# The last channel block of a depthwise convolution moved to diagonal matrices on TensorE, and LayerNorm operations pinned by block

## The chip, the cores and the metric

One NeuronCore of one Trainium2 chip. The metric is the device time of one execution in microseconds (us). Engines: TensorE (PE) multiplies matrices, VectorE (DVE) and ScalarE (ACT) work element by element, GpSimd (POOL) does small operations and issues some transfers, SyncE (SP) issues the other transfers.

## The reference

One layer of a decoder on 512 tokens and 16 learned meta tokens in front of them, 1024 channels, float32. A mixing sub-layer: RMSNorm; one input projection whose columns go to a Mamba-2 state-space group (SSD, 16 heads, chunks of 128) and to a Conformer convolution group; the outputs of both, 2048 channels, pass one output projection, and the result is added to the stream. A channel sub-layer: RMSNorm, then retrieval over 128 x 128 experts (PEER). A last RMSNorm; the meta tokens are dropped. The part that the change touches:

```python
def conformer_conv(u, conv_w, conv_b, ln_g, ln_b):
    a, g = jnp.split(u, 2, axis=-1)
    h = causal_depthwise_conv(a * jax.nn.sigmoid(g), conv_w, conv_b)   # width 31, 1024 channels
    hf = h.astype(jnp.float32)
    mu = jnp.mean(hf, axis=-1, keepdims=True)
    var = jnp.mean(jnp.square(hf - mu), axis=-1, keepdims=True)
    hn = (hf - mu) * lax.rsqrt(var + EPS) * ln_g.astype(jnp.float32) + ln_b.astype(jnp.float32)
    return jax.nn.silu(hn).astype(u.dtype)
```

## The kernel before, in words

The program is one straight line of instructions; each engine's order is fixed when the program is built, by a list scheduler that runs a simulated time line. `early(n)` raises the priority of what stands in it by n, `late(n)` lowers it. Every matrix product is done as three matmuls in float32r (`mm3`, lines 160 to 162): each factor is split into a high part and a low remainder, and high x high, high x low and low x high are summed in PSUM. Lines 160, 161 and 162 in the profile are therefore those of all products.

Weights: `wload` (line 167) loads a raw block of 1 MB through SP's queue into one of two places. `wsplit` (line 176) copies it on ACT as the high part (line 184), again with its sign turned (line 185), and adds the raw block to that copy by an accumulating transfer on POOL's queue (line 186): the low part. The split parts too have two places, used in turn; a place is free when PE has done the matmuls on the block that was in it.

Input projection (lines 588 to 597): blocks z, x and c run in the order of the list `ORDER`, whose last entries are c6 and c7. `x_block` feeds SSD; `ssd(g)`, four groups of five chunks, runs with priority 2000 on all engines. `c_block(k)` (line 406) is one block of 128 convolution channels with all 528 tokens: two projections, the gate (tanh form of the sigmoid), `gl` = 14 zeros and 528 gated values, then the convolution with lowered priority: one ACT scaling (line 420) and 30 taps on DVE (line 422), each adding a shifted `gl` times a column of weights to the block's 512 columns. Then the mean of block 0 (`crow`) is taken off, and the sums `sumd` and `sumq` over blocks are kept for LayerNorm (lines 424 to 441); block 7 enters the statistics on its own (`sq7`).

SSD's results of groups 0 to 2 go through memory (`yD`) and are transposed and split into the left factors of the output projection (`y_group`, `y_split`: line 620 on PE, 626 on ACT, 627 on DVE; priority 300). `out_part([0])` and `out_part([1])` project SSD's 1024 channels, each in two halves of 512 output columns and 96 matmuls; line 653 adds a finished half to the stream. Between them and `out_part([2, 3])`, which projects the convolution's 1024 channels, stands LayerNorm (lines 672 to 696, priority 500): sums over channels by matmuls with ones (line 676), a few small operations, two matmul broadcasts to rows (line 402), and for each block k two DVE operations (691, 692), the swish and the high copy on ACT (693, 695), and the low part on DVE (696). These parts are written to the places `hl(k)`, which the left factors of `out_part([0])` (k = 0 to 3) and `out_part([1])` (k = 4 to 7) held. Behind `out_part([2, 3])` come the second RMSNorm (lines 701 to 714), the PEER queries and scores, and two long loops over experts (`down`, `up_mm`), also products in three matmuls.

Of the kernel before, what the change touches and what calls it, by code (L numbers as in the profile page):

```python
# [9 lines left out]
F32 = mybir.dt.float32  # L10
# [5 lines left out]
AF = mybir.ActivationFunctionType  # L16
OP = mybir.AluOpType
# [25 lines left out]
TB = 8  # L43
ORDER = "z0 c0 x4 c1 x5 x6 c2 x7 x0 z1 x1 c3 c4 z2 x2 c5 z3 x3 c6 c7".split()
YP = 300
MO = (0, 1, -1, 2, 3)


# [2 lines left out]
S_CW, S_CB, S_LG, S_LB, S_SW, S_SB = 0, 248, 256, 264, 272, 336  # L51
# [4 lines left out]
def consts_array():  # L56
    c = np.zeros((128, C_N), np.float32)
    p = np.arange(128)
    c[:, C_ID:C_ID + 128] = np.eye(128)
    c[:, C_TRI:C_TRI + 128] = p[:, None] <= p[None, :]  # L60
    c[:, C_IOTA:C_IOTA + 128] = p[None, :]
    c[:, C_I50:C_I50 + 50] = np.arange(50)[None, :]
    return c


def pack(inputs):
    g = {k: np.asarray(v) for k, v in inputs.items()}
    ac = np.ascontiguousarray
    w_in = g["w_in"][0]
    zc, xbc, dtc, ca, cg = 0, 1024, 3072, 3088, 4112  # L70
    blocks = []
    for k in range(1, 4):
        blocks.append(w_in[:, zc + 256 * k:zc + 256 * k + 256])
    for k in range(8):
        blocks.append(w_in[:, xbc + 256 * k:xbc + 256 * k + 256])
    for k in range(8):
        blocks.append(np.concatenate([w_in[:, cg + 128 * k:cg + 128 * k + 128],
                                      w_in[:, ca + 128 * k:ca + 128 * k + 128]], 1))
    wb = np.stack(blocks)
    win = ac(wb.reshape(19, 8, 128, 2, 128).transpose(0, 2, 3, 1, 4))  # L80
    wzdt = np.concatenate([w_in[:, zc:zc + 256], w_in[:, dtc:dtc + 16]], 1)
    wzdt = ac(wzdt.reshape(8, 128, 272).transpose(1, 0, 2))
    w_out = g["w_out"][0]
    wout = ac(w_out.reshape(4, 4, 128, 2, 512).transpose(3, 0, 2, 1, 4))
    wq = ac(g["peer_w_query"][0].reshape(8, 128, 8, 256).transpose(2, 1, 0, 3))
    keys = np.stack([g["peer_sub_keys_1"][0], g["peer_sub_keys_2"][0]], 1)
    keysT = ac(keys.transpose(3, 0, 1, 2).reshape(128, 16, 128))
    wd, wu = g["peer_w_down"][0], g["peer_w_up"][0]
    wdT = ac(wd.reshape(128, 128, 8, 128).transpose(0, 3, 2, 1))
    cc = lambda a: a.reshape(-1, 128).T  # L90
    small = np.concatenate([
        g["conf_conv_w"][0].reshape(31, 8, 128).transpose(2, 1, 0).reshape(128, 248),
        cc(g["conf_conv_b"][0]), cc(g["conf_ln_g"][0]), cc(g["conf_ln_b"][0]),
        g["ssd_conv_w"][0].reshape(4, 16, 128).transpose(2, 1, 0).reshape(128, 64),
        cc(g["ssd_conv_b"][0]), cc(g["ssd_norm_w"][0])], 1)
    rowb = np.concatenate([g["ssd_dt_bias"][0], g["ssd_A_log"][0], g["ssd_D"][0]])
    nw = np.stack([g["norm_mix_w"][0], g["ssd_norm_w"][0], g["norm_ffn_w"][0], g["norm_final_w"]])
    return dict(x=ac(g["x"][0]), meta=ac(g["meta_tokens"]), win=win, wzdt=wzdt, wout=wout, wq=wq,
                keysT=keysT, wdT=wdT, wd=ac(wd), wu=ac(wu), small=ac(small), rowb=ac(rowb), nw=ac(nw),
                cst=consts_array())  # L100


# [15 lines left out]
def body(ctx, tc, I, out):  # L118
    nc = tc.nc
    V, S, G, E = nc.vector, nc.scalar, nc.gpsimd, nc.tensor  # L120
# [7 lines left out]
    def ps(tag="pb"):  # L128
        return psp.tile([128, 512], F32, name=tag, tag=tag)
# [4 lines left out]
    def late(n):  # L134
        return tc.high_priority(offset=-n)

    def mem(a, n):
        assert a + n <= SLAB
        return M[:, a:a + n]
# [7 lines left out]
    def con(n):  # L147
        a = cp[0]
        cp[0] += n
        assert cp[0] <= W0, cp[0]  # L150
        return M[:, a:a + n]
# [43 lines left out]
    cst = con(C_N)  # L195
# [18 lines left out]
    small = con(S_N)  # L214
# [11 lines left out]
    rowb = con(48)  # L226
# [64 lines left out]

    for n, t in enumerate(MO):
        src, c0, parts = (xt[t], NM + 128 * t, 128) if t >= 0 else (xm, 0, NM)
# [6 lines left out]
        for half in range(2):  # L300
            hs = slice(512 * half, 512 * half + 512)
            V.scalar_tensor_tensor(u[:, hs], src[:parts, hs], r, wmix[:parts, hs], op0=OP.mult, op1=OP.mult)
            p = ps("pa" if n % 2 else "pb")
# [81 lines left out]
    convo = mem(V0, 4096).rearrange("p (c t) -> p c t", c=8)  # L385
    glu = [mem(F0 + 544 * k, 544) for k in range(4)]
    sig = mem(F0 + 2176, 528)
    atmp = [mem(F0 + 2704 + 512 * k, 512) for k in range(2)]
    cwh = con(248)
    V.tensor_scalar(cwh, small[:, S_CW:S_CW + 248], 0.5, None, op0=OP.mult)  # L390
    crow = mem(L0, 512)
    sumd = mem(L0 + 512, 512)
    sumq = mem(L0 + 1024, 512)
    assert L0 + 1536 <= SLAB
    ccol = con(4)
    atn = [0]
    sq7 = []

    def to_rows(cols):
        p = ps()  # L400
        for t in range(4):
            E.matmul(p[:, 128 * t:128 * t + 128], cols[:, t:t + 1].to_broadcast([128, 128]), ident,
                     start=True, stop=True)
        return p

    def c_block(k):
        wh, wl = next_w()
        g0, g1 = proj_ct(wh, wl, 0)
        S.activation(sig[:, 0:272], g0[:, :272], AF.Tanh, scale=0.5)
        S.activation(sig[:, 272:528], g1[:, :256], AF.Tanh, scale=0.5)  # L410
        a0, a1 = proj_ct(wh, wl, 1)
        gl = glu[k % 4]
        if k < 4:
            V.memset(gl[:, 0:14], 0.0)
        V.scalar_tensor_tensor(gl[:, 14:286], sig[:, 0:272], 1.0, a0[:, :272], op0=OP.add, op1=OP.mult)
        V.scalar_tensor_tensor(gl[:, 286:542], sig[:, 272:528], 1.0, a1[:, :256], op0=OP.add, op1=OP.mult)
        o = convo[:, k, :]
        cw = cwh[:, 31 * k:31 * k + 31]
        with late(LOWP):
            S.activation(o, gl[:, 0:512], AF.Identity, scale=cw[:, 0:1], bias=small[:, S_CB + k:S_CB + k + 1])  # L420
            for j in range(1, 31):
                V.scalar_tensor_tensor(o, gl[:, j:j + 512], cw[:, j:j + 1], o, op0=OP.mult, op1=OP.add)  # L422
            if k > 0:
                V.tensor_tensor(o, o, crow, op=OP.subtract)
            if k == 0:
                p = ps()
                for t in range(4):
                    E.matmul(p[:, t:t + 1], o[:, 128 * t:128 * t + 128], ones[:, 0:1], start=True, stop=True)
                V.tensor_scalar(ccol, p[:, 0:4], 1.0 / 128, None, op0=OP.mult)
                S.activation(crow, to_rows(ccol), AF.Copy)  # L430
                V.tensor_tensor(o, o, crow, op=OP.subtract)
                S.activation(sumq, o, AF.Square)
            else:
                at = atmp[atn[0] % 2]
                atn[0] += 1
                S.activation(at, o, AF.Square)
                if k < 7:
                    V.tensor_tensor(sumq, sumq, at, op=OP.add)
                    V.tensor_tensor(sumd, convo[:, 0, :] if k == 1 else sumd, o, op=OP.add)
                else:  # L440
                    sq7.append(at)


    sm = con(80 * 12)
# [157 lines left out]
    def hl(kk):  # L602
        g = RG[kk // 4]
        return g[0][:, kk % 4, :], g[1][:, kk % 4, :]
# [49 lines left out]

    with early(YP):
        def y_group(g):
# [15 lines left out]
    with early(LNP):  # L672
        p = ps()
        for c0, src in ((0, sumd), (4, sumq), (8, convo[:, 7, :]), (12, sq7[0])):
            for t in range(4):
                E.matmul(p[:, c0 + t:c0 + t + 1], src[:, 128 * t:128 * t + 128], ones[:, 0:1], start=True, stop=True)
        mom = stat(8)
        V.tensor_scalar(mom, p[:, 0:8], 1.0 / D, None, op0=OP.mult)
        V.scalar_tensor_tensor(mom, p[:, 8:16], 1.0 / D, mom, op0=OP.mult, op1=OP.add)
        dl = mom[:, 0:4]  # L680
        vv = stat(4)
        V.tensor_tensor(vv, dl, dl, op=OP.mult)
        V.tensor_tensor(vv, mom[:, 4:8], vv, op=OP.subtract)
        rst = rstd_of(vv, 4, 1.0)
        rho = stat(4)
        V.tensor_tensor(rho, dl, rst, op=OP.mult)
        prh = to_rows(rho)
        prs = to_rows(rst)
        for k in range(8):
            cv = convo[:, k, :]  # L690
            V.tensor_tensor(cv, cv, prs, op=OP.mult)
            V.tensor_tensor(cv, cv, prh, op=OP.subtract)
            S.activation(cv, cv, AF.Silu, bias=small[:, S_LB + k:S_LB + k + 1], scale=small[:, S_LG + k:S_LG + k + 1])
            ch, cl = hl(k)
            S.activation(ch, cv, AF.Copy)  # L695
            V.tensor_tensor(cl, cv, ch.bitcast(F32), op=OP.subtract)

    wffn = mem(P0, 1024)
    load(wffn, bcast(I["nw"][2], 1024))
# [110 lines left out]
    for h in range(8):  # L810
        wh, wl = split_n(raw_n(I["wq"][h].rearrange("p c n -> p (c n)"), 2048), 2048, V)
        for f in range(2):
            pq = ps("pa")
            for dc in range(8):
                o = dc * 256 + f * 128
# [246 lines left out]
        final(m)  # L1062


ARRAYS = ["x", "meta", "win", "wzdt", "wout", "wq", "keysT", "wdT", "wd", "wu", "small", "rowb", "nw", "cst"]


# [13 lines left out]
```

## Time and profile before

| what | value |
|---|---|
| median of three runs | 1674.62 us (1671.99 to 1677.26) |
| the profiled execution | 1675.73 us, span 1674.0 us, mean granted clock 0.985 |
| busy: PE, DVE, ACT, POOL | 97%, 83%, 46%, 23% of the span |
| bytes read from memory | 381.7 MB |

The span goes from the first to the last instruction. A row of the time line has the start, the duration, the engine, the line, the operation, what it writes and reads, and in square brackets how long the engine was idle before it and what ended that. Matmuls overlap in the pipeline, so the distance of their starts is their pace, not the duration. The granted clock is the share of TensorE's full clock (2.4 GHz) that the chip gave; 0.50 is 1.2 GHz.

### The profile page before, as it was taken

The page shows a single profiled execution, that of the slowest core. Times are in us where ns is not written, and L with a number is a line of the kernel's source. Part 1 is how long each engine was busy: PE and PEld are TensorE (multiplying, and loading weights), DVE is VectorE, ACT ScalarE, POOL GpSimd, SP SyncE. Part 2 cuts the span into 40 slices and gives each one's busy share as a digit, 9 for nine tenths or more (in the row PEclk, how much of TensorE's full clock was granted, in tenths as well). Part 3 has the DMA queues.
Part 4 walks back from the last instruction along what each step waited for, and adds up shares of the span by engine and source line. Part 5 has one row for each costly group of instructions (what it writes and reads, how often), then busy time and mean ns, then how long its engine had stood idle before and what let it go on. Part 6 is the DMA issues. An engine that isn't in the chain of part 4 may idle for free. (4 is left out here: it accounts for less than half of the span.)

```text
span 1674.0 us, 26115 instructions
## 1 busy us (share of the span) xinstructions
PE 1620.4 (97%) x9529; PEld 1471.2 (88%) x9529; DVE 1395.3 (83%) x2864; ACT 769.5 (46%) x1155; POOL 390.2 (23%) x336
## 2 busy tenths in 40 slices
PE   7999999887899999999999999999999999999997
PEld 7999999666788999999999988888888899999996
DVE  5999899994478998999998478888888888888876
ACT  5566566535423344567676333333333333333333
POOL 1111111000000002012233232222222355464430
PEclk9999999987999999999999999999999999999999
DMA  7877576654322356699999889999999899999982
GB/s 219 192 170 167 127 161 162 197 133 101 106 82 100 125 188 230 206 329 342 329 326 322 298 289 360 357 334 359 342 344 349 303 343 353 357 351 368 340 311 97
DMA packets 165185, 425.38 MB, mean 254 GB/s; under 512 B 14384, under 2 KB 81200, under 8 KB 159424
## 3 DMA queue, kind: packets, MB, share of 16 engines
q1 hardware_dynamic: 121568, 261.17, 44.8%
q0 software_dynamic: 43488, 162.55, 31.9%
q8 instruction: 74, 1.21, 0.3%
q14 instruction: 55, 0.45, 0.1%
HBM read 381.72 MB, written 41.94 MB: 253 GB/s over the span
## 5 line engine op out<-in xcount | busy, mean ns | idle before, releaser
L160 PE MATMUL pa<-MR 128*128 128x512 f32 (+3 forms) x2120 | 727.5, 344 | 13.8 <-ACT MR L695 7.6
L161 PE MATMUL pa<-MR 128*128 128x512 f32 (+3 forms) x2120 | 726.7, 343 | 1.0 <-DMA MR<-wout 1.0
L162 PE MATMUL pa<-MR 128*128 128x512 f32 (+3 forms) x2120 | 687.6, 343 | 1.1 <-DVE MR L267 1.0
L160 PEld LDWEIGHTS pa<-MR 128*128 128x128 f32 x2120 | 402.5, 190 | 45.1 <-ACT MR L695 7.9
L161 PEld LDWEIGHTS pa<-MR 128*128 128x128 f32 x2120 | 401.9, 190 | 31.1 <-DMA MR<-wout 1.4
L162 PEld LDWEIGHTS pa<-MR 128*128 128x128 f32 x2120 | 400.9, 189 | 32.0 <-DVE MR L267 1.2
L773 ACT ACTIVATE MR<-M 128x1024 fp32r<-128x1024 f32 (+1 forms) x264 | 285.9, 1084 | 297.9 <-PE pa L161 104.9
L774 DVE TENSOR_TENSOR MR<-M,MR 128x1024 fp32r<-128x1024 f32 (+1 forms) x264 | 330.2, 1252 | 77.2 <-ACT MR L773 71.6
L914 POOL DMA_INDIRECT M<-wd,M x128 | 160.0, 1250 | 548.8 <-DVE M L930 283.2
L914 POOL DMA_INDIRECT M<-wu,M x128 | 168.3, 1315 | 308.8 <-DVE M L937 264.3
L161 PE MATMUL pb<-MR 128*128 128x384 f32 (+1 forms) x576 | 206.8, 359 | 0.0
L160 PE MATMUL pb<-MR 128*128 128x384 f32 (+1 forms) x576 | 206.3, 359 | 0.0
L162 PE MATMUL pb<-MR 128*128 128x384 f32 (+1 forms) x576 | 204.2, 359 | 0.0
L1001 ACT ACTIVATE MR<-M 128x384 fp32r<-128x384 f32 x128 | 67.0, 523 | 274.8 <-issue 203.5
L422 DVE SCALAR_TENSOR_TENSOR M<-M 128x512 f32<-128x512 f32 x240 | 173.7, 746 | 3.9 <-ACT M L420 3.0
L937 DVE SCALAR_TENSOR_TENSOR M<-M 128x1024 f32<-128x1024 f32 x128 | 163.7, 1279 | 15.6 <-DMA M<-wu,M 15.3
L930 DVE SCALAR_TENSOR_TENSOR M<-M 128x1024 f32<-128x1024 f32 x128 | 154.1, 1219 | 10.1 <-DMA M<-wd,M 10.0
L1002 DVE TENSOR_TENSOR MR<-M,MR 128x384 fp32r<-128x384 f32 x128 | 71.2, 556 | 59.9 <-ACT MR L1001 59.2
L161 PEld LDWEIGHTS pb<-MR 128*128 128x128 f32 x576 | 108.1, 188 | 11.3
L160 PEld LDWEIGHTS pb<-MR 128*128 128x128 f32 x576 | 108.1, 188 | 11.3
L162 PEld LDWEIGHTS pb<-MR 128*128 128x128 f32 x576 | 108.1, 188 | 10.8
L976 ACT ACTIVATE M<-pb 128x512 f32<-128x512 f32 x96 | 98.9, 1159 | 37.5 <-PE pb L974 37.5
(221 smaller groups left out, 1469.5 us busy)
## 6 DMA issues: line engine op xcount, KB each, us to landing
M<-wdT SPq DMA_DIRECT2D x128, 512.0 KB
M<-wu SPq DMA_DIRECT2D x128, 512.0 KB
GD<-M SPq DMA_DIRECT2D x40, 512.0 KB
M<-GD SPq DMA_DIRECT2D x32, 640.0 KB
M<-win SPq DMA_DIRECT2D x19, 1024.0 KB
MR<-win POOLq DMA_DIRECT2D x38, 512.0 KB
HD<-M SPq DMA_DIRECT2D x88, 192.0 KB
M<-HD SPq DMA_DIRECT2D x88, 192.0 KB
```

What stands on the lines that cost most here:

```text
L160: E.matmul(o, lh, rh, start=first, stop=False)
L161: E.matmul(o, lh, rl, start=False, stop=False)
L162: E.matmul(o, ll, rh, start=False, stop=last)
L422: V.scalar_tensor_tensor(o, gl[:, j:j + 512], cw[:, j:j + 1], o, op0=OP.mult, op1=OP.add)
L773: S.activation(wh, raw, AF.Copy)
L774: leng.tensor_tensor(wl, raw, wh.bitcast(F32), op=OP.subtract)
L914: r = G.indirect_dma_start(out=g, out_offset=None, in_=src, in_offset=bass.IndirectOffsetOnAxis(ap=e3[:, k:k + 1], axis=0))
L930: use(V.scalar_tensor_tensor(g, g, 1.0, x2s, op0=OP.mult, op1=OP.mult, accum_out=dots[:, k:k + 1]))
L937: use(V.scalar_tensor_tensor(h1[3], g, act3[:, k:k + 1], h1[3], op0=OP.mult, op1=OP.add))
L976: S.activation(gb.rearrange("p i t -> p t i")[:, c:c + 4, :], p.rearrange("p (t i) -> p t i", t=4), AF.Copy, scale=1.0 / GS)
L1001: S.activation(sh, sf, AF.Copy)
L1002: V.tensor_tensor(sl, sf, sh.bitcast(F32), op=OP.subtract)
```

## The change

For block 7 the 30 taps and the scaling are replaced by `c_diag`: `gl` is split into a high and a low part (`gh`, `gw`); 31 diagonal matrices, one for each tap, are prepared on the host (`cdiag`, two blocks of 1 MB, the second with 15 matrices and one of zeros), and loaded and split like the other weights, in two halves each. Each diagonal multiplies the 512 columns of `gl` from its shift on, in three matmuls that add up in one PSUM tile: 93 matmuls. ACT scales the sum by 0.5 and adds the bias. The rest of the block stays. The loads stand in program order behind c7's block and ahead of the first block of `wout`. `early(DGP)` with DGP = 0 changes no priority.

In LayerNorm the DVE operations are traced block by block, with the low part of block k - 2 behind the first two operations of block k, and each is pinned behind the DVE operation that was traced before it, so that the scheduler can't change their order among themselves. The operations and their number stay.

```diff
@@ -43,6 +43,7 @@
 TB = 8
 ORDER = "z0 c0 x4 c1 x5 x6 c2 x7 x0 z1 x1 c3 c4 z2 x2 c5 z3 x3 c6 c7".split()
 YP = 300
+DGP = 0
 MO = (0, 1, -1, 2, 3)
 
 
@@ -93,10 +94,13 @@
         cc(g["conf_conv_b"][0]), cc(g["conf_ln_g"][0]), cc(g["conf_ln_b"][0]),
         g["ssd_conv_w"][0].reshape(4, 16, 128).transpose(2, 1, 0).reshape(128, 64),
         cc(g["ssd_conv_b"][0]), cc(g["ssd_norm_w"][0])], 1)
+    cdiag = np.zeros((2, 128, 16, 128), np.float32)
+    for j in range(31):
+        cdiag[j // 16, np.arange(128), j % 16, np.arange(128)] = g["conf_conv_w"][0].reshape(31, 1024)[j, 896:]
     rowb = np.concatenate([g["ssd_dt_bias"][0], g["ssd_A_log"][0], g["ssd_D"][0]])
     nw = np.stack([g["norm_mix_w"][0], g["ssd_norm_w"][0], g["norm_ffn_w"][0], g["norm_final_w"]])
     return dict(x=ac(g["x"][0]), meta=ac(g["meta_tokens"]), win=win, wzdt=wzdt, wout=wout, wq=wq,
-                keysT=keysT, wdT=wdT, wd=ac(wd), wu=ac(wu), small=ac(small), rowb=ac(rowb), nw=ac(nw),
+                keysT=keysT, wdT=wdT, wd=ac(wd), wu=ac(wu), small=ac(small), rowb=ac(rowb), nw=ac(nw), cdiag=cdiag,
                 cst=consts_array())
 
 
@@ -416,6 +420,9 @@
         V.scalar_tensor_tensor(gl[:, 286:542], sig[:, 272:528], 1.0, a1[:, :256], op0=OP.add, op1=OP.mult)
         o = convo[:, k, :]
         cw = cwh[:, 31 * k:31 * k + 31]
+        if k == 7:
+            c_diag(gl, o)
+            return
         with late(LOWP):
             S.activation(o, gl[:, 0:512], AF.Identity, scale=cw[:, 0:1], bias=small[:, S_CB + k:S_CB + k + 1])
             for j in range(1, 31):
@@ -434,11 +441,26 @@
                 at = atmp[atn[0] % 2]
                 atn[0] += 1
                 S.activation(at, o, AF.Square)
-                if k < 7:
-                    V.tensor_tensor(sumq, sumq, at, op=OP.add)
-                    V.tensor_tensor(sumd, convo[:, 0, :] if k == 1 else sumd, o, op=OP.add)
-                else:
-                    sq7.append(at)
+                V.tensor_tensor(sumq, sumq, at, op=OP.add)
+                V.tensor_tensor(sumd, convo[:, 0, :] if k == 1 else sumd, o, op=OP.add)
+
+    def c_diag(gl, o):
+        gh, gw = memr(16960, 544)[:, 0:542], memr(17504, 544)[:, 0:542]
+        split_to(gh, gw, gl[:, 0:542])
+        p = ps("pa")
+        for q in range(2):
+            src = I["cdiag"][q].rearrange("p j n -> p (j n)")
+            wh, wl = wsplit(wload(src), src, parts=2)
+            for j in range(16 - q):
+                ds = slice(128 * j, 128 * j + 128)
+                t0 = 16 * q + j
+                mm3(p, wh[:, ds], wl[:, ds], gh[:, t0:t0 + 512], gw[:, t0:t0 + 512], t0 == 0, t0 == 30)
+        with early(DGP):
+            S.activation(o, p, AF.Identity, scale=0.5, bias=small[:, S_CB + 7:S_CB + 8])
+            V.tensor_tensor(o, o, crow, op=OP.subtract)
+            at = atmp[atn[0] % 2]
+            S.activation(at, o, AF.Square)
+            sq7.append(at)
 
 
     sm = con(80 * 12)
@@ -686,14 +708,22 @@
         V.tensor_tensor(rho, dl, rst, op=OP.mult)
         prh = to_rows(rho)
         prs = to_rows(rst)
+        pin = tc.keep_in_program_order
+
+        def low(k):
+            ch, cl = hl(k)
+            pin(V.tensor_tensor(cl, convo[:, k, :], ch.bitcast(F32), op=OP.subtract))
+
         for k in range(8):
             cv = convo[:, k, :]
-            V.tensor_tensor(cv, cv, prs, op=OP.mult)
-            V.tensor_tensor(cv, cv, prh, op=OP.subtract)
+            pin(V.tensor_tensor(cv, cv, prs, op=OP.mult))
+            pin(V.tensor_tensor(cv, cv, prh, op=OP.subtract))
             S.activation(cv, cv, AF.Silu, bias=small[:, S_LB + k:S_LB + k + 1], scale=small[:, S_LG + k:S_LG + k + 1])
-            ch, cl = hl(k)
-            S.activation(ch, cv, AF.Copy)
-            V.tensor_tensor(cl, cv, ch.bitcast(F32), op=OP.subtract)
+            S.activation(hl(k)[0], cv, AF.Copy)
+            if k > 1:
+                low(k - 2)
+        low(6)
+        low(7)
 
     wffn = mem(P0, 1024)
     load(wffn, bcast(I["nw"][2], 1024))
@@ -1062,7 +1092,7 @@
         final(m)
 
 
-ARRAYS = ["x", "meta", "win", "wzdt", "wout", "wq", "keysT", "wdT", "wd", "wu", "small", "rowb", "nw", "cst"]
+ARRAYS = ["x", "meta", "win", "wzdt", "wout", "wq", "keysT", "wdT", "wd", "wu", "small", "rowb", "nw", "cdiag", "cst"]
 
 
 def kernel(**inputs):
```

## Rows read from the trace of the kernel before

**Rows 1.** The page's 40 slices of 41.85 us, busy tenths, engines PE and DVE

```profile
PE   7999999887899999999999999999999999999997
...
DVE  5999899994478998999998478888888888888876
```

**Rows 2.** PE's waits from 460 us to the end: total, times, longest

```profile
PE pb L899 <- DVE M L859: 1.5, 1, 1.5
...
PE pa L160 <- ACT MR L773: 0.9, 1, 0.9
```

**Rows 3.** PE's waits from 298.2 to 438.9 us

```profile
PE pa L620 <- DVE MR L627: 9.6, 5, 4.7
PE pa L160 <- ACT MR L695: 7.6, 1, 7.6
PE pa L160 <- DVE MR L627: 2.5, 1, 2.5
PE pb L402 <- DVE M L686: 2.5, 1, 2.5
...
PE pa L620 <- DVE M L653: 0.9, 1, 0.9
PE pb L559 <- DVE M L549: 0.4, 1, 0.4
```

**Rows 4.** Windows: us, busy PE, PEld, DVE, ACT, POOL (instructions), granted clock, DMA share, GB/s

```profile
298.20:438.90 140.70, 116.08 (x531) 94.94 (x531) 101.34 (x204) 63.58 (x108) 10.69 (x14) 0.88 0.50 131
...
304.40:310.40 6.00, 3.98 (x18) 3.88 (x19) 5.14 (x12) 2.19 (x7) 0.00 (x0) 0.50 1.06 245
...
344.80:354.70 9.90, 6.14 (x17) 4.22 (x18) 9.90 (x25) 4.21 (x14) 1.19 (x2) 0.50 0.69 148
...
379.40:396.20 16.80, 7.69 (x26) 6.61 (x27) 11.63 (x21) 8.51 (x12) 1.95 (x2) 0.51 0.50 126
```

**Rows 5.** Time line of PE in out_part([1])

```profile
351.02 0.80 PE L160 MATMUL pa<-MR 128*128 128x512 f32 x1 [2.53 <-DVE MR L627]
...
352.04 0.63 PE L162 MATMUL pa<-MR 128*128 128x512 f32 x1
352.47 0.63 PE L160 MATMUL pa<-MR 128*128 128x512 f32 x1
...
356.83 0.39 PE L162 MATMUL pa<-MR 128*128 128x512 f32 x1
...
371.11 0.39 PE L162 MATMUL pa<-MR 128*128 128x512 f32 x1
```

**Rows 6.** DVE from 298 to 374.5 us: window, group of taps, seven taps in the time line

```profile
298.00:374.50 76.50, 62.98 (x300) 50.96 (x299) 75.39 (x154) 33.72 (x68) 5.92 (x8) 0.89 0.56 154
...
L422 DVE SCALAR_TENSOR_TENSOR M<-M 128x512 f32<-128x512 f32 x62 | 44.6, 746 | 0.0
...
352.98 4.72 DVE L422 SCALAR_TENSOR_TENSOR M<-M 128x512 f32<-128x512 f32 x7
```

**Rows 7.** Time line, DVE and PE, from block 7's last tap to out_part([2, 3])

```profile
373.79 0.69 DVE L424 TENSOR_TENSOR M<-M 128x512 f32<-128x512 f32 x1
...
384.67 4.87 DVE L691 TENSOR_TENSOR M<-M,pb 128x512 f32<-128x512 f32 x8 [3.94 <-PE pb L402]
...
392.26 0.79 PE L160 MATMUL pa<-MR 128*128 128x512 f32 x1 [7.63 <-ACT MR L695]
```

**Rows 8.** Weight splits: the group of 1024-column copies, and one wout block's time line

```profile
L184 ACT ACTIVATE MR<-M 128x1024 fp32r<-128x1024 f32 x38 | 39.9, 1062 | 13.9 <-PE pa L161 13.3 <-PE pa L162 0.7
...
405.19 1.92 ACT L184 ACTIVATE MR<-M 128x2048 fp32r<-128x2048 f32 x1 [5.09 <-PE pa L162]
...
409.35 0.86 POOL L186 DMA_DIRECT2D MR<-wout  x1 [27.53 <-ACT MR L185]
...
417.24 0.50 PE L161 MATMUL pa<-MR 128*128 128x512 f32 x1 [0.98 <-DMA MR<-wout]
```

**Rows 9.** Time line of PE behind the output projection

```profile
445.22 1.09 PE L611 MATMUL pb<-M 128*128 128x128 f32 x4 [4.39 <-DVE M L709]
```

## The prediction

> **What bounds the kernel now.** I read the page's busy shares and its 40 slices first [rows 1]. TensorE (PE) is busy in nine tenths or more of most slices, except in numbers 7 to 10 counted from 0, which is 293 to 460 us; there it falls to 7 and 8 tenths, while VectorE (DVE) stands at 9 until slice 8. Then I read PE's waits behind 460 us [rows 2]: three of 1.5, 1.4 and 0.9 us (the first and the last stand there), 3.8 in all of 1214. So from 460 us to the end the kernel runs at PE's pace, and what the front saves comes off the end one for one, as long as the static order behind it doesn't change much.
>
> The front is the stretch from the last matmul of block c7's projection (298.2 us) to the last matmul of the output projection (438.9). PE's waits there [rows 3] add up to 24.5 us: 9.6 + 0.9 in the transposes of the SSD rows (line 620) and 2.5 + 0.4 beside them, 2.5 and 7.6 on the LayerNorm chain, and a last one of 1.0 on a weight transfer. The windows [rows 4] say the same: 116.1 us busy in 140.7. They also show three stretches in which the granted clock is 0.50, the lower of its two levels (1.2 of 2.4 GHz), each one following such a wait; PE is busy there for 3.98 + 6.14 + 7.69 = 17.8 us. The pace at either level is in the matmul rows [rows 5]: at full clock 63 matmuls of 512 columns take 371.11 - 356.83 = 14.28 us, 0.2267 each; at the low level one takes 0.43. So about half of 17.8, 8.9 us, is clock loss, and the front's pure matmul work is 116.1 - 8.9 = 107.2 us in a stretch of 140.7.
>
> What it waits for is DVE: from 298 to 374.5 us DVE is busy for 75.4 of 76.5 us [rows 6], and 62 of its operations are convolution taps (line 422).
>
> **The change, part by part.** *Removed from DVE:* 30 taps of block 7. Seven in a row take 4.72 us [rows 6], so one follows another by (4.72 - 0.75)/6 = 0.66 us, and 30 of them are 19.9 us; by the mean duration of 746 ns, which overlaps the neighbour, it would be 22.4. I take 19.9. One ScalarE (ACT) scaling of 0.8 us goes too. *Added to DVE:* the low half of gl, one subtraction over 542 columns, some 0.7 us. The subtraction of crow and ACT's square stay.
>
> *Added to PE:* 31 taps x 3 = 93 matmuls of 512 columns, 93 x 0.2267 = 21.1 us at full clock, 40.0 at the low one. I take full clock, since they fill the first hole, in front of which the clock is still full. The Trainium skill ("TensorE: Matmul & The Clock Gate", section "Back-to-back issue gap") gives N/2.4 + 2.5 ns for a lone stream, 216 ns, and about 131 ns sustained; 93 of them would be 20.1 or 12.2 us and the gain 1.0 or 8.9 us larger. The trace doesn't agree: with weight loads beside them such matmuls keep to 0.2267 us.
>
> *The sum on PE:* 107.2 + 21.1 = 128.3 us of work against a stretch of 140.7. If no wait and no low clock is left, the gain is 12.4 us, and in this stretch it can't be more. That the DVE loses 20 us is not the gain: the gain is what holes PE has, less what it is given.
>
> *Do the holes close?* First hole (4.7 us, the longest of line 620's waits, and the low clock from 304.4 behind it): cdiag's first half is loaded and split in the place that wout's first block had, before 298, so the diagonal matmuls can start when gl is there and split: one operation on ACT, one on DVE, during which the SSD matmuls that run now go on. Bounds 0 and 3; I allow 1 us. Second hole: before, the last transposed SSD rows are there at 351.02 [rows 5]. PE's work up to there is 52.8 us less the waits 9.6 + 0.9 + 0.4 + 2.5 = 13.4 and about 3 of low clock, 36.4; with 21.1 more PE comes there at 298.2 + 57.5 + 1 = 356.7. Even if the SSD chain gets no faster, its 351 is hidden by 5.7 us. If that cover were gone the hole would cost what it does now, up to 7.5 us and its clock. Third hole: the LayerNorm chain runs from the end of block 7's taps to the first matmul of out_part([2, 3]), 373.8 to 392.26 us [rows 7], 18.5 us. With 62 - 30 taps left, DVE's queue reaches the end of the convolution some 19 us sooner, near 355; the chain would be ready near 373, while PE, with some 26 us of work (351 to 378, less the clock loss) still in front of it, is at out_part(1) until about 382. It is hidden by 9 us, and the DVE part that the cover needs is short.
>
> *The pinned LayerNorm order:* the same 24 DVE and 16 ACT operations, by block instead of by kind. Before, the 16 first ones stand in two runs of 8 (4.87 us each, 0.61 an operation [rows 7]), and the first block is ready 4.9 + 0.6 us behind the first of them; by block it is 1.2. That is worth up to 4.3 us where the chain is on the path, and nothing where it is hidden by 9 us; I put it at 0. What the pin can cost: behind the low half of block 4, which waits for out_part([1]) to leave its operand's place, DVE's queue holds blocks 6 and 7 back. DVE needs 3 x 0.61 = 1.8 us a block, PE 12 x 0.2267 = 2.7, so DVE keeps ahead: 0. At the other end, if PE had to wait for all of blocks 4 to 7, it would be 4 x 1.8 = 7.3 us.
>
> *Weights and queues.* Two loads of 1 MB on SP's queue and four accumulating transfers of 512 KB on POOL's come in front of wout's, and eight copies of 1.06 us on ACT (8.5 us, by the rows of the 1024-column splits [rows 8]); ACT is busy 63.6 of 140.7 us [rows 4], so they cost 0 directly. But each wout block now waits for a place that a diagonal half holds, not a projection block. The cycle of a place is in [rows 8]: from the first copy at 405.19 over the issue at 409.35 to PE's start at 417.24, 12.05 us; PE's work on the other place is 48 x 0.2267 = 10.9 plus what lies between. In that execution it cost 0.98 us once in four blocks, 0.25 a block. Bounds for eight blocks: 0 (something always lies between) and 8 x 1.1 = 9. I take 2, by the row. What is queued behind these copies on ACT, the SSD exponentials and the copies of line 626, can be held up when the static order, made by a simulated time line, has put them late; for that and other misplacements I allow 1 us, bounds 0 and 5.
>
> *Result:* 12.4 - 1 - 2 - 1 = 8.4 us. Against the profiled execution's 1675.7 us (span 1674.0) that is 1667.3; against the median 1674.62, which is what counts, 1666.2.
>
> **The rivals.**
> *(a) The waits change their names.* The holes are filled by the diagonals, but the weight ring or the static order makes new ones: 9 us for the ring and 3 to 5 more for the order, so that the gain is -1 to 5: 1670 to 1676. For it: there is no slack between 12.05 and 10.9 us. Against it: before, four blocks in a row lost 1.0 us.
> *(b) Slower: the moving operand's start.* gh[:, t0:t0+512] starts at every single element, and no matmul before does so (offsets 0, 16 + 128t, 272, multiples of 512). If odd starts were read at half the pace, each would take 0.43 us, PE's work grow by 93 x 0.203 = 18.9 us, and the result be 8.4 - 18.9 = 10.5 us slower, 1685. It decides from 0.2267 + 12.4/93 = 0.36 us a matmul. Against it: the 240 taps read odd starts on DVE, and their durations lie together. The Trainium skill ("SBUF — State Buffer", "Operand start alignment") allows any start at a multiple of the element, and says that its runs timed nothing; no row here shows it for PE.
> *(c) More than the stretch.* Behind 438.9 PE waits another 4.39 us for line 709's chain [rows 9]. If the new order puts DVE's splits (line 774), which mix with that chain, otherwise, that wait goes too: 8.4 to 12.4 and 4.4 more, 1658 to 1662.
> *(d) It doesn't do what it says:* the order keeps PE waiting for SSD as now, and the diagonals come as pure addition, or something late in the queue order changes: 0 to 10 us slower, 1675 to 1685.
>
> **How the numbers follow.** Forecast (gain 5 to 12.4) 0.58, (a) 0.18, (b) 0.08, (c) 0.10, (d) 0.06. The likeliest is 1666.2. The range 1658 to 1676 takes in the forecast, (a), (c) and the ring's bounds; (b) and half of (d), 0.11, lie outside, and some 0.05 of misjudged ends. A measurement of this kernel tells 0.3%, 5 us, from no change. Faster than 1669.6: the forecast and (c), 0.68. Within: (a) and a third of (d), 0.20. Slower: (b) and the rest of (d), 0.12.
>
> **What would show it.** Right: matmuls of 0.227 us from about 301 to 325 us, where the 4.7 us wait was; no clock under 1 between 300 and 430; the waits of lines 620 and 160 on DVE and ACT gone, those on wout's transfers 1 to 3 us; statistics matmuls (line 676) among out_part([1])'s; the last output projection matmul near 430. Wrong: diagonal matmuls spaced by more than 0.36 us; waits on wout of over 5 us; a LayerNorm chain that still ends behind out_part([1]); or the front shorter by 8 us and the total not, which would mean that the order behind 460 us has changed.

## The result, and the profile after

The changed kernel takes 1683.35 us (median of 6 executions, 1682.09 to 1684.27) against 1674.63 for the kernel before on the same chip: 1.0053 times as long, 95% interval 1.0042 to 1.0063, so 8.7 us slower where 8.4 us faster was forecast. The profiled execution takes 1684.21 us with a span of 1682.4. The lines of the kernel have moved: the three matmuls of a product are lines 164 to 166 (before 160 to 162), the transposes of the SSD rows line 642 (620), the two halves of their split lines 648 and 649 (626 and 627), the LayerNorm's 719 to 722 and 715, the addition of the output projection 675, the transposes behind it 633 (611).

The 40 slices, PE and DVE, against [rows 1]:

```profile
PE   7999999889899999999999999999999999999997
...
DVE  5999899763469999999998468888888889888876
```

DVE has fallen from 9, 9, 4 and 4 tenths to 7, 6, 3 and 4 in slices 7 to 10, counted from 0, as meant, and PE is not full for all that: in numbers 7, 8 and 10 it still stands at 8. The front ends, on PE, where the 16 transposes behind the output projection begin, and they begin 9.56 us later than before (438.92):

```profile
448.48 1.91 PE L633 MATMUL pb<-M 128*128 128x128 f32 x16
```

So the whole loss was made in the front, and what followed it came later by about as much (the span is 8.4 us longer). PE's waits from 290 to 470 us (total, times, longest), against [rows 3]:

```profile
PE pa L642 <- DMA M<-yD: 7.0, 1, 7.0
PE pa L642 <- DVE MR L649: 6.7, 2, 4.5
PE pb L633 <- DVE M L739: 4.4, 1, 4.4
PE pa L165 <- DMA MR<-wout: 2.1, 5, 0.7
PE pb L561 <- ACT M L587: 0.4, 1, 0.4
```

The wait of 7.6 us on the LayerNorm is gone. But the transposes of the SSD rows wait for 13.7 us, more than before (10.5, and 1.6 on yD just ahead of the stretch of [rows 3]), once on a load and twice until the split of earlier ones has emptied a tile. Leaving out line 633's, which lies behind the front, PE waits for 16.2 us, where it had waited for 24.5. The stretch, and its three parts at the lower granted clock (us, then busy us of PE, PEld, DVE, ACT, POOL, granted clock, DMA share, GB/s), against [rows 4]:

```profile
295.90:448.48 152.58, 136.36 (x629) 111.14 (x628) 85.48 (x180) 70.32 (x114) 14.84 (x17) 0.93 0.58 147
303.00:310.50 7.50, 2.91 (x8) 2.46 (x9) 3.65 (x10) 1.16 (x4) 0.00 (x0) 0.55 0.68 177
361.70:368.90 7.20, 7.20 (x30) 6.42 (x30) 2.06 (x9) 2.56 (x4) 1.03 (x1) 0.53 0.11 22
375.00:382.00 7.00, 4.24 (x11) 3.47 (x12) 6.96 (x16) 6.62 (x15) 0.00 (x0) 0.53 0.50 101
```

About half of 2.91 + 7.20 + 4.24, 7.2 us, is lost to the clock, an estimate from the two paces. So PE's work at full clock is 136.4 - 7.2 = 129.2 us; 128.3 was forecast. Waits and clock together cost 16.2 + 7.2 = 23.4 us, where the forecast had left 4.0 of the 33.4 before. The sum of the work was right; that the holes would close was wrong.

*The first hole*, on PE's time line (start, us, what, and in brackets how long it had been idle and on whom):

```profile
299.60 0.58 PE L164 MATMUL pa<-MR 128*128 128x512 f32 x1
300.02 0.60 PE L642 MATMUL pa<-M 128*128 128x128 f32 x4
307.59 0.66 PE L642 MATMUL pa<-M 128*128 128x128 f32 x2 [6.98 <-DMA M<-yD]
...
311.06 0.39 PE L164 MATMUL pa<-MR 128*128 128x512 f32 x1
...
314.56 0.40 PE L164 MATMUL pa<-MR 128*128 128x512 f32 x1
```

The first diagonal matmul runs at 299.60, so its operands were there in time. Then PE's own order brings the transposes of group 0's rows 0 and 1, and those of row 2 stand in front of all the other diagonals (92 of the 93 matmuls). Row 2's load is late. SP's queue, POOL's, and the window from 295 to 300 us:

```profile
297.07 0.33 SPq L158 DMA_DIRECT2D M<-wout  x1
297.49 0.40 SPq L158 DMA_DIRECT2D M<-yD  x1
```

```profile
298.44 0.90 POOL L190 DMA_DIRECT2D MR<-cdiag  x1 [1.25 <-ACT MR L189]
```

```profile
295.00:300.00 5.00, 4.58 (x31) 3.50 (x31) 5.00 (x13) 3.83 (x7) 1.55 (x2) 1.00 1.04 276
```

A row of 128 KB, issued at 297.49 behind 1 MB of wout and beside 512 KB of cdiag, with the DMA share at 1.04, lets PE go on only at 307.59.

*The second hole*, PE, then ACT, then ACT in the kernel before, then DVE:

```profile
358.90 4.21 PE L698 MATMUL pb<-M 128*128 128x1 f32 x32
366.10 1.48 PE L642 MATMUL pa<-M 128*128 128x128 f32 x6
...
372.27 0.95 PE L642 MATMUL pa<-M 128*128 128x128 f32 x6 [2.14 <-DVE MR L649]
...
377.76 0.69 PE L642 MATMUL pa<-M 128*128 128x128 f32 x2 [4.53 <-DVE MR L649]
```

```profile
346.58 0.51 ACT L599 ACTIVATE M<-M 128x256 f32<-128x256 f32 x1 [1.90 <-POOL M L263]
```

```profile
346.03 0.51 ACT L577 ACTIVATE M<-M 128x256 f32<-128x256 f32 x1
```

```profile
352.74 0.69 DVE L675 TENSOR_TENSOR M<-M,pa 128x512 f32<-128x512 f32 x1 [0.63 <-PE pa L166]
...
366.34 0.69 DVE L675 TENSOR_TENSOR M<-M,pa 128x512 f32<-128x512 f32 x1 [0.89 <-PE pa L166]
```

The last SSD row is finished by ACT at 347.1, half a microsecond later than in the kernel before (346.5). The 16 transposes of groups 2 and 3 run from 366 to 378, where before the last of them had been split and used at 351.02 [rows 5]. They write PSUM tiles named pa, of which there are four, and out_part([0]), ahead of them in the program, takes all four for its second half; the additions that read these out run from 352.74 to 366.34. Behind that the transposes, which need ACT and DVE to empty each tile, fall together with the pinned LayerNorm on the same two engines.

### The profile page after: what moved, and what is told of

Its sections match the earlier page's. It is cut to its first block, busy times and chain, and to the rows that moved or that the text cites. A ratio compares the mean times of both kernels' runs of the same rounds, so it can differ in the third digit from the quotient of the medians.

```text
span 1682.4 us, 26300 instructions
## 1 busy us (share of the span) xinstructions
PE 1639.9 (97%) x9622; PEld 1487.3 (88%) x9622; DVE 1378.3 (82%) x2835; ACT 777.5 (46%) x1164; POOL 391.2 (23%) x340
## 5 line engine op out<-in xcount | busy, mean ns | idle before, releaser
L164 PE MATMUL pa<-MR 128*128 128x512 f32 (+3 forms) x2151 | 738.8, 345 | 3.7 <-ACT M L826 1.4
L165 PE MATMUL pa<-MR 128*128 128x512 f32 (+3 forms) x2151 | 740.0, 344 | 2.1 <-DMA MR<-wout 2.1
L166 PE MATMUL pa<-MR 128*128 128x512 f32 (+3 forms) x2151 | 702.0, 345 | 1.2 <-DVE MR L271 1.1
L164 PEld LDWEIGHTS pa<-MR 128*128 128x128 f32 x2151 | 408.4, 190 | 35.7 <-ACT MR L270 2.0
L165 PEld LDWEIGHTS pa<-MR 128*128 128x128 f32 x2151 | 408.3, 190 | 35.1 <-DMA MR<-wout 4.3
L166 PEld LDWEIGHTS pa<-MR 128*128 128x128 f32 x2151 | 407.6, 190 | 33.0 <-DVE MR L271 1.3
L967 DVE SCALAR_TENSOR_TENSOR M<-M 128x1024 f32<-128x1024 f32 x128 | 163.7, 1279 | 14.9 <-DMA M<-wu,M 14.6
L429 DVE SCALAR_TENSOR_TENSOR M<-M 128x512 f32<-128x512 f32 x210 | 153.1, 747 | 3.3 <-ACT M L427 2.3
L165 PEld LDWEIGHTS pb<-MR 128*128 128x128 f32 x576 | 108.1, 188 | 11.3
L164 PEld LDWEIGHTS pb<-MR 128*128 128x128 f32 x576 | 108.1, 188 | 11.3
```

The source lines that it names most:

```text
L164: E.matmul(o, lh, rh, start=first, stop=False)
L165: E.matmul(o, lh, rl, start=False, stop=False)
L166: E.matmul(o, ll, rh, start=False, stop=last)
L967: use(V.scalar_tensor_tensor(h1[3], g, act3[:, k:k + 1], h1[3], op0=OP.mult, op1=OP.add))
```

## The experiments

Every kernel was timed against the kernel before on its own chip; medians of that were 1674.07 (e_notaps, e_pinonly, e_nopin, e_onemm), 1674.31 (e_hold, e_ydfirst, e_pb, e_pb_before) and 1673.68 (the last four). A difference between two kernels of the table is taken from their medians below. By the ratios, the three gains on the changed kernel that the argument rests on (6.9, 5.3 and 10.3 us for e_hold, e_ydfirst and e_pb) are 7.2, 4.7 and 9.7 us, each known to about 2.5 us.

| kernel | us | ratio to before, 95% |
|---|---|---|
| changed | 1683.35 | 1.0053 [1.0042, 1.0063] |
| e_notaps | 1665.6 | 0.9951 [0.9934, 0.9967] |
| e_pinonly | 1670.47 | 0.9982 [0.9972, 0.9991] |
| e_nopin | 1690.83 | 1.0096 [1.0079, 1.0113] |
| e_onemm | 1670.75 | 0.9978 [0.9967, 0.9989] |
| e_hold | 1676.49 | 1.0010 [0.9999, 1.0020] |
| e_ydfirst | 1678.02 (nine of ten: 1673.48 to 1682.99; one 2330.81) | 1.0025 [1.0013, 1.0037] |
| e_pb | 1673.03 | 0.9995 [0.9984, 1.0005] |
| e_pb_before | 1675.47 | 1.0011 [1.0001, 1.0021] |
| e_hold_pb | 1666.52 | 0.9950 [0.9931, 0.9969] |
| e_hold_pb_yd | 1666.54 | 0.9958 [0.9946, 0.9970] |
| e_hold_pb_nopin | 1668.71 | 0.9970 [0.9959, 0.9981] |
| e_high | 1662.04 | 0.9927 [0.9910, 0.9945] |

**The parts by themselves.** First the removal alone: the kernel before with block 7's 30 taps left out and nothing in their place.

```diff
-            for j in range(1, 31):
+            for j in range(1, 31 if k < 7 else 1):
```

> The kernel before, without the 30 VectorE taps of block 7 (that block's convolution is left out but for its first tap) and with nothing put on TensorE in their place. It shows what VectorE's relief alone is worth. Theory A, that only the LayerNorm wait (2.5 + 7.6 us and its low clock, about 14 us) hangs on VectorE's queue, and that the waits on the SSD rows' transposes have other causes (PSUM tiles of out_part, loads of yD): about 1660 to 1663 us, the waits of line 620 on line 627 still 8 us or more. Theory B, on which the prediction rested, that VectorE's taps make all three holes: 1641 to 1648 us, line 620's waits under 3 us.

It is 8.5 us faster. Its waits from 290 to 470 us:

```profile
PE pa L161 <- DMA MR<-wout: 4.8, 2, 3.9
...
PE pa L620 <- DVE M L424: 4.4, 1, 4.4
PE pa L620 <- DVE MR L627: 4.3, 2, 4.1
PE pa L620 <- DMA M<-yD: 1.7, 1, 1.7
```

Without these taps the LayerNorm's 7.6 us go. The transposes of line 620 still wait for 10.7 us, with one more of 0.3 (12.1 before, in the same stretch); 8.7 of them end on DVE's lines 424 and 627. So block 7's taps made the third hole, not the first two. The run's windows show why (columns as in [rows 4], DVE's busy time the third):

```profile
298.00:345.00 47.00, 38.03 (x187) 31.07 (x187) 45.26 (x102) 26.37 (x58) 5.77 (x7) 0.87 0.61 170
345.00:375.00 30.00, 28.67 (x132) 23.95 (x131) 14.91 (x35) 8.50 (x12) 1.96 (x2) 0.80 0.41 99
```

Up to 345 us DVE is busy for 45.3 of 47.0 us with other work, the taps of earlier blocks among it. The relief comes behind that (14.9 of 30.0), when the second hole is nearly over (its last wait ends at 347.5). Whether fewer taps further ahead would close the first two holes was not tried. Theory A is the nearer one, but neither came as written: 1665.6 us lies between the two ranges, line 620 waits for 4.3 us on line 627 and not for 8, and the waits on wout have grown from 1.0 to 4.8 us.

Then the pin alone (the kernel before with the changed LayerNorm loop), and the changed kernel with the LayerNorm loop of before:

> The kernel before with the pinned LayerNorm order alone, taps on VectorE as before. Here the LayerNorm chain is on the path, so the order by block should shorten it: theory A, the pin does no harm: 1668 to 1672 us, TensorE's wait on line 695 down from 7.6 to 3 or 4 us. Theory C, that the pins are what made the changed kernel slow (they hold VectorE's queue for the last SSD rows): 1675 to 1682 us.

> The changed kernel with LayerNorm's operations traced and free as before: block 7 by diagonals alone. Theory A, that the loss comes from 21 us of matmuls against holes that closed only in part: 1682 to 1687 us, the pin being worth 0 to 4. Theory C, that the pins delay the last SSD rows: 1672 to 1678 us, with line 642's waits on line 649 (6.7 us) gone.

The pin alone is worth 3.6 us, in theory A's range, and in the changed kernel 7.5. The wait on the LayerNorm in e_pinonly, which was 7.6 before:

```profile
PE pa L160 <- ACT MR L700: 3.0, 1, 3.0
```

and what grows without it in e_nopin, where it was 6.7 in the changed kernel:

```profile
PE pa L642 <- DVE MR L649: 11.3, 2, 6.7
```

So the theory that the pin does the harm, by holding the splits of line 649 back, falls (theory C, in both runs). Theory A's 0 to 4 us for the pin in the changed kernel were too few too, and e_nopin lies above its range. The diagonals with everything that comes with them cost 1690.83 - 1665.6 = 25.2 us without the pin, known to about 4: what their 93 matmuls take (93 x 0.2333 = 21.7) or more, so on balance nothing of them went into a hole.

Next, how much of a matmul counts: the changed kernel with the product of the high parts alone, so that 62 of the 93 matmuls and with them the low parts' share of the sum are left out.

```diff
-  mm3(p, wh[:, ds], wl[:, ds], gh[:, t0:t0 + 512], gw[:, t0:t0 + 512], t0 == 0, t0 == 30)
+  E.matmul(p, wh[:, ds], gh[:, t0:t0 + 512], start=t0 == 0, stop=t0 == 30)
```

> The changed kernel with one matmul for each tap, high by high, in place of three; the other two products of block 7 are left out. 62 matmuls less, 62 x 0.2327 = 14.4 us of TensorE's time; the loads, splits and order stay. Theory A, that the matmuls lie on the path from end to end: 1668 to 1671 us. Theory D, that they mostly fill time in which TensorE waits for transfers and transposes anyhow: 1678 to 1683 us.

12.6 us of 62 x 0.2333 = 14.5 come out at the end, in theory A's range. But the order did not stay as it was, against what was expected: the scheduler put 22 of the 31 matmuls in front of the transposes of row 2, where the changed kernel has one of 93. The first ran at 299.61, the others here (the diagonals are line 457):

```profile
300.38 5.12 PE L457 MATMUL pa<-MR 128*128 128x512 f32 x21
```

The wait of 7.0 us on yD is gone with that, 1.5 us on DVE stand in its place, and there are new waits, of 3.9 us at the statistics and 2.1 us at an SSD matmul; from 290 to 470 us PE waits for 14.5 us, line 633 left out, against 16.2. So this run doesn't tell how much of a matmul counts in the order of the changed kernel; for that e_nopin against e_notaps is the evidence.

**The two holes.** e_hold leaves all work as it is and puts one order on PE: the transposes of group 0's rows 2 and 3 come behind the products of the 12th tap.

```diff
-            E.transpose(p[:, d * 128:d * 128 + 128], src[:, d * 128:d * 128 + 128], ident)
+            r = E.transpose(p[:, d * 128:d * 128 + 128], src[:, d * 128:d * 128 + 128], ident)
+            if g0 == 0 and t > 1:
+                behind(r, dg[HOLDN])      # HOLDN = 11
```

> The changed kernel, with one constraint more on TensorE's order: the transposes of SSD group 0's third and fourth rows stand behind the twelfth diagonal. In the changed kernel they stood in front of all but one diagonal matmul, and TensorE waited 7.0 us there for a load of yD, then 8 us at the low clock. Theory A1, that the diagonals could have filled that wait but stood behind it: 1674 to 1677 us, the wait on yD gone and the clock full until 358 us. Rival, that the diagonals can't start there either (gl's split, cdiag's transfers): 1681 to 1684 us, a wait of the first diagonals in its place.

It is 6.9 us faster than the changed kernel, as theory A1 had it; the wait on yD is gone, and the granted clock is 1.00 from 300 to 350 us. The second hole stays:

```profile
PE pa L650 <- DVE MR L659: 6.5, 3, 3.2
```

e_ydfirst goes at the same hole from the other end: PE's order is free, and SP issues the load of wout's second half behind those of rows 2 and 3.

```diff
+                raw = wload(src)
+                if b == 0 and hf == 1:
+                    behind(wl_[0], yl[3])
```

> The changed kernel, with the load of wout's second block (1 MB on SP's queue, not needed before 330 us) put behind the loads of yD's third and fourth rows; TensorE's order stays. Theory A2, that this block, with the cdiag transfers, stands in front of the awaited 128 KB in the transfer engines: the wait shrinks from 7.0 to 2 to 4 us, 1677 to 1680 us. Rival, that the wait comes from when the row is written or its place is free: no change, 1682 to 1685 us.

SP's queue (rows 2 and 3, then wout), and the transposes' wait on yD:

```profile
296.08 0.33 SPq L158 DMA_DIRECT2D M<-yD  x1
...
297.92 0.47 SPq L158 DMA_DIRECT2D M<-yD  x1
298.44 0.43 SPq L158 DMA_DIRECT2D M<-wout  x1
```

```profile
PE pa L648 <- DMA M<-yD: 0.3, 1, 0.3
```

Row 2's load is issued at 296.08, 1.41 us sooner than in the changed kernel; 1.06 of that is a shift of the whole trace (line 583's matmuls at 295.91 there, the same ones at 294.85 here). With 1 MB less in front of it the row is there in time: 0.3 us of wait instead of 7.0, where theory A2 had left 2 to 4, and 5.3 us in the end. The wait on the split (line 655 there) stays, at 7.5 us. Two different cures for one wait, each worth 5 to 7 us, show that it was this load, behind the megabyte, with the diagonals behind it in PE's order.

e_pb gives the transposes of groups 2 and 3 PSUM tiles of the other name, and nothing else.

```diff
-        p = ps("pa")
+        p = ps("pb" if g0 >= 2 else "pa")
```

> The changed kernel, with the transposes of SSD groups 2 and 3 in PSUM tiles of the other kind (pb), so that they need not wait until out_part([0]) gives its four tiles (pa) back. In the changed kernel the last group's rows were ready at 347 us, but their transposes stood at 366 to 378, with 6.7 us of waits and some 4 us of low clock. Theory A3, that the tiles hold them back: they move in among out_part([0])'s matmuls, the waits on the low parts' line go under 2 us, 1674 to 1678 us. Rival, that ScalarE's and VectorE's LayerNorm operations, which now run in the same place, make the wait: 1681 to 1684 us.

10.3 us faster than the changed kernel, 1 us better than theory A3's range. The wait on line 649 is gone, the one on yD stays at 6.5, and on PE's time line 10 of the 16 transposes now run inside out_part([0]) (the other 6 beside the statistics, from 360 to 364):

```profile
334.55 0.38 PE L642 MATMUL pb<-M 128*128 128x128 f32 x2
347.97 0.27 PE L642 MATMUL pb<-M 128*128 128x128 f32 x1
348.32 0.93 PE L642 MATMUL pb<-M 128*128 128x128 f32 x7
```

The same edit in the kernel before:

> The kernel before with the same change of PSUM tiles. There the last rows are ready only at 346.5 us, and out_part([0]) ends at 339.5. Theory A3: group 2's transposes move ahead of 339.5 and group 3's follow their rows; of the 7.5 us of waits 2 to 4 go, 1668 to 1673 us. Rival, that SSD's chain alone sets 351 us: 1673 to 1677 us.

No gain: 1.1 thousandths slower, just clear of no change. That is the rival's range, but not its reason, since the second hole closes there too, and PE waits elsewhere:

```profile
PE pa L160 <- ACT MR L695: 7.6, 1, 7.6
PE pb L676 <- DVE M L439: 5.6, 1, 5.6
...
PE pb L676 <- DVE M L424: 1.4, 1, 1.4
```

It now waits for 7.0 us at the statistics, until DVE has brought the convolution's sums and block 7 (lines 439 and 424), and then for the LayerNorm as long as ever (7.6 as in [rows 3]). So before the change the hole of the tiles was slack under another chain, DVE's taps and the LayerNorm behind them, and closing it was worth nothing. The change took that chain away, and what had been slack became the path. Whether the same holds of the first hole was not tried in the kernel before.

**Together.**

> The changed kernel with both repairs: the third and fourth rows' transposes behind the twelfth diagonal, and the transposes of groups 2 and 3 in the other PSUM tiles. Theory A, that the two waits are separate and TensorE is paced by nothing else: the gains of 6.9 and 10.3 us add up, 1664 to 1669 us, faster than the kernel before. Rival, that the LayerNorm chain or the weight places come next and take one of them back: 1671 to 1674 us.

1683.35 - 6.9 - 10.3 would be 1666.15; 1666.52 was measured, 7.2 us under the kernel before, in theory A's range. That this is 0.3 us from the forecast's time doesn't confirm the forecast, which was for the change without these two repairs. The largest wait in the front, and the stretch:

```profile
PE pa L166 <- DMA MR<-wout: 2.9, 2, 1.8
```

```profile
295.27:430.61 135.34, 131.55 (x628) 108.56 (x627) 84.64 (x180) 70.17 (x114) 15.60 (x17) 0.97 0.64 167
```

3.8 us of waits are left in the front: the weight ring's 2.9, 0.5 for the low half of gl and 0.4 for ACT. The row that held PE for 7 us is issued no earlier than in the changed kernel, the shift of the trace taken off (296.86 here, 0.6 us sooner, as is all around it): PE has other work meanwhile. This version is faster than both kernels.

e_hold_pb_yd adds e_ydfirst's order to it, e_hold_pb_nopin takes the pin out:

> The same two repairs, and wout's second block loaded behind the rows of yD. Theory A: the diagonals hide the load already, so no change against the two repairs, 1664 to 1669 us. Rival, that the early transfers also cost elsewhere (the second diagonal block, out_part([0])'s first block): 2 to 4 us faster.

> The same two repairs with LayerNorm's operations free. Without the repairs the pin was worth 7.5 us in the changed kernel. Theory A, that it was worth that only where LayerNorm's operations ran beside the last transposes: with those moved away the pin is worth under 2 us, 1665 to 1670 us. Rival, that the pin shortens a chain that is still on the path: 1671 to 1676 us.

The first changes nothing (1666.54): behind 12 taps of diagonals the load is hidden anyway. The second costs 2.2 us, where theory A had under 2. The intervals of the two ratios overlap, so these runs don't settle whether the pin still helps.

Last, what limits the repaired kernel: e_hold_pb_yd with the product of the high parts alone, the low parts of the taps and of gl left out, and the transposes held behind the 28th tap.

> The two repairs and wout's second block behind yD, and of block 7's three products only high by high: the low parts of gl and of cdiag, their transfers and copies and 62 matmuls are left out. 62 x 0.2327 = 14.4 us of TensorE's time. Theory A, that TensorE's work is now the pace of the whole front: 1651 to 1655 us. Rival, that with less on TensorE the LayerNorm chain or the transposes come out again: 1658 to 1664 us.

Only 4.5 of the 14.5 us come out, where e_onemm had given 12.6: the rival's range. Its waits:

```profile
PE pb L571 <- ACT M L597: 4.6, 1, 4.6
...
PE pb L591 <- DVE M L271: 2.3, 1, 2.3
PE pa L166 <- DMA MR<-wout: 2.0, 3, 1.4
```

The two new ones, 4.6 (it was 0.4) and 2.3 us, are not those that the rival named. They are the SSD chain's own matmuls, which wait until ACT has copied the chain's state (line 597) and for DVE (line 271). The front of e_hold_pb_yd, and of e_high:

```profile
294.00:429.63 135.63, 131.70 (x643) 108.83 (x642) 86.41 (x182) 70.26 (x116) 15.64 (x17) 0.99 0.65 170
```

```profile
294.00:426.25 132.25, 122.24 (x580) 99.74 (x579) 86.17 (x181) 69.92 (x115) 18.31 (x16) 0.95 0.62 167
```

PE is idle for 10.0 us in place of 3.9, and its busy time has fallen by 9.5 us only, at a clock of 0.95 in place of 0.99. So in the repaired kernel the diagonals do fill time that PE could not use otherwise; with a third of them the SSD chain is next. How much of this is due to the other place of the hold was not tried apart.

## Why the prediction was wrong

- *PE bounds the kernel, the front comes off the end one for one.* Right: the front ends 9.6 us later, the total is 8.7 longer; in e_hold_pb 8.3 sooner and 7.2 shorter.
- *PE's work, 128.3 us.* Right: 129.2. The pace of the added matmuls measured (314.56 - 311.06)/15 = 0.2333 us against 0.2267, which is 0.6 us for 93. The Trainium skill's 216 and 131 ns ("TensorE: Matmul & The Clock Gate", section "Back-to-back issue gap") would have been further off, as the rows of before had said.
- *"What it waits for is DVE."* Too wide, though the sum didn't rest on it: it put three holes down to one busy engine. Taking 30 taps from DVE (e_notaps) closed the LayerNorm hole alone; the transposes waited for 10.7 us instead of 12.1, since the relief comes behind 345 us.
- *"The diagonal matmuls can start when gl is there and split"; 1 us for the first hole.* The first failed step. They could start, and one did, at 299.60. The step failed in asking when operands are ready and not what stands ahead on PE's queue: the order put group 0's transposes in front, and their load behind 1 MB of wout. 7.0 us of wait and some 1.5 of clock. The text had named the cause, "misplacements" by the static order, and given it 1 us with a bound of 5; e_hold measured 6.9 us where the hole and the misplacements together had 2.
- *"Even if the SSD chain gets no faster, its 351 is hidden by 5.7 us."* The second failed step, and the dearest (10.3 us by e_pb). The last row was there at 347.1, 0.6 us later than before, so the rows are not what failed. But 351.02 of before was the end of a chain that includes transposes on PE and two engines emptying their tiles, and PE arrives at these when its order and the four pa tiles let it: behind out_part([0]), which the 21 us of diagonals had moved back as well. A moment that depends on PE's own progress can't be held fixed while PE is given more work.
- *LayerNorm chain hidden by 9 us.* Right: no wait on it in the changed kernel, nor in e_hold_pb, where PE comes there without the two holes.
- *The pin at 0.* Mis-sized: 3.6 us gain before, 7.5 in the changed kernel, 2.2 in the repaired one (the last not clear of the noise). "Nothing where it is hidden" left out that ACT and DVE were also to empty the transposes' tiles meanwhile, where the wait on line 649 is 11.3 us without the pin and 6.7 with it.
- *Weight ring 2 us.* Right: 2.1, and 2.9 in e_hold_pb.
- *The rivals.* (b) falls: odd starts are read at 0.2333 us. (a) had the right kind, waits that change their names, and named the static order, but with 3 to 5 us; the ring, its larger part, didn't come. (c) falls: the wait behind the front stays at 4.4 us. (d), "the order keeps PE waiting for SSD as now, and the diagonals come as pure addition", 1675 to 1685, is nearest to what happened, with e_nopin's 25.2 us for 21.7 of matmuls behind it; but not in full, since the LayerNorm hole closed, and only the other two kept PE waiting. It had 0.06. It should have had most of what the forecast had: nothing in the trace of before showed where PE's order would put 93 new instructions.

That PE's order was made with an earlier time for that load than the chip gave is the likely reason for the first hole, but it is argued: y_group has the priority 300 and c_diag's matmuls none, and no trace shows the times that the scheduler reckoned with.

## What to carry to other kernels

A hole in an engine is filled by new work only if the new work stands in front of the waiting instruction in that engine's static order; so for each hole, name the instruction that waits, what it needs (input, PSUM tile, queue place), and what stands behind it. Before a chain is removed, look for holes that are slack under it, since they become the path afterwards: a cure that was worth nothing before (e_pb_before) was then worth 10 us (e_pb). And a "ready at" time taken from a trace may be kept fixed only if nothing in its chain runs on the engine that gets the new work.

## What the runs showed of the hardware

The granted clock fell without any wait of PE. In e_hold_pb, PE is busy without a gap from 350 to 360 us and the clock of that stretch is 0.77; the window, and the time line about the fall:

```profile
350.00:360.00 10.00, 10.00 (x56) 9.10 (x55) 3.46 (x13) 5.54 (x9) 1.51 (x2) 0.77 0.84 209
```

```profile
353.16 4.82 PE L708 MATMUL pb<-M 128*128 128x1 f32 x32
...
358.53 0.63 PE L166 MATMUL pa<-MR 128*128 128x512 f32 x1
358.95 0.63 PE L167 MATMUL pa<-MR 128*128 128x512 f32 x1
```

The fall comes with the 32 statistics matmuls of one column each, which take 4.82 us; behind them the 512-column matmuls follow one another by 0.42 us, the pace of the lower level [rows 5]. The changed kernel shows the same from 361.7 on, within its line 698, where 7.2 busy us ran at 0.53; so does e_pb (0.66 from 364 to 369 us, PE busy for all of it). Half of the 7.2, 3.6 us by estimate, is lost to the lower level there, and no wait shows it. That the one-column matmuls are the reason is likely, and was not tried apart.

A load of 128 KB held PE for 7.0 us when it was queued behind 1 MB with the DMA share at 1.04; issued ahead of that megabyte, and 0.4 us sooner by its own trace's clock (e_ydfirst), it held PE for 0.3.
